# One more duo of F tiles in block products, and a new order of side work: a change to a two-layer convolution and pooling trunk

## The chip, the cores and the metric

The kernel runs on one core of one Trainium2 chip. The metric is device time of one execution in microseconds. The core has five engines that run their own instruction streams and wait for each other by semaphores: TensorE (PE: matmuls, and the weight loads PEld beside them), VectorE (DVE), ScalarE (ACT), GpSimd (POOL) and SyncE (SP). In this kernel SP issues most transfers; POOL's queue issues the rest, all those that add to what stands at their destination among them.

## The reference

Two residual layers over 1024 positions of 1024 channels, conditioned by a vector c. Each has a token mixer (layer 0: a causal convolution of width 31 with a gate and a layer norm; layer 1: pooled means) and a SwiGLU feed-forward part of width 2816.

```python
c_act = silu(c)
for i in range(2):
    sh_m, sc_m, g_m, sh_f, sc_f, g_f = split(c_act @ ada_w[i] + ada_b[i], 6)
    h = modulate(rms_norm(x, norm_mix_g[i]), sh_m, sc_m)
    y = conformer_conv(h, ...) if i == 0 else multiscale_pool(h, ...)
    x = x + (1 + g_m) * y
    h = modulate(rms_norm(x, norm_ffn_g[i]), sh_f, sc_f)
    x = x + (1 + g_f) * ((silu(h @ w_gate[i]) * (h @ w_up[i])) @ w_down[i])
return rms_norm(x, final_g)
```

All of it is float32. On the chip each operand of a large product is split in a high part (rounded to PE's fast float type) and a low part (the rest), and a product is three matmuls: high by high, high by low, low by high.

## The kernel before

**Tiling.** The sequence is cut in two chunks A and B of 512 positions; channels lie on the 128 partitions, so a tile is 128 x 512. F has 22 tiles, counted in 11 pairs `fp` (one gate and up product of 256 columns each) and 6 duos `q` (two pairs; the last has one). `products` (L506) issues the three matmuls of one product. `load_weight` (L489) loads a weight block, casts its high part on ACT and makes its low part on DVE or POOL or, with `summed`, as a negated copy on ACT to which a POOL transfer adds the block from memory.

**Block products.** The down product of the feed-forward part multiplies, for each duo, a 2 x 2 block matrix of weights (odd or even tiles, lower or upper half of the channels) with a 2 x 2 block matrix of activations (tiles by chunks). Instead of eight block products, seven are enough where sums and differences of blocks are formed first. Layer 1 does so for all duos. Layer 0 does it from pair `BEGINS[0]` on, which is 8: duos 4 and 5, F tiles 16 to 21. The tiles below are multiplied classically, the even tiles of chunk A already in the heads.

**Stages of layer 0.** (1) The first product of the convolution (`conv_in`), with the depthwise taps on DVE and POOL beside it (`Taps`, L800: POOL's share goes by a product on ACT and a sum on POOL). (2) The layer norm of chunk A (`layer_norm_silu`, L874), the second product `conv_out`, and the feed-forward norm of A (`norm`, L655; `modulated`, L645: a scaling on DVE, a high part on ACT, a low part on DVE, for each of eight channel tiles). Beside them `ada_columns` (L447) makes four of the modulation vectors of layer 0 by products of one column, a load of 512 KB for each of 32. (3) `heads` (L2024): two rounds of four pairs, each followed by a `down` (L1425) of A's even tiles, with the rest of B's taps and B's layer norm beside them. `gated` (L1061) applies the gate and splits the result. (4) `conv_out` of B and `all_joint` (L2042): for each pair the remaining head products, of which `joint` (L1212) ends each either by `gated`, which writes split tiles to memory, or by `paired` (L1268), which forms the operands of the block products and writes three blocks. (5) `first_down` (L1606): steps a and b (A's odd tiles, classical), p2, p1, p6, p7, p4, p5, p3 (block products), c to f (B, classical). Beside them run the pooling of layer 1 for A and the modulation of layer 1 (`ada_task`, L401).

**Side work of a block product step.** `weights` (L1639) forms and splits the weight block; `operand` (L1503) loads an activation block, casts the high part on ACT and subtracts it on DVE for the low part. `prepare` (L1679) loads operands four steps ahead and splits them two steps ahead; their parts stand in a ring of eight buffers (tag `h0`), two to a step.

**Order.** PE's order is the program's. For the other engines, work is emitted as tasks that `pace` (L234) steps while a model clock of DVE or POOL is less than 4 us ahead of PE's; `yield` names in `LOAD` and `DELAY` (L55, L71) say how long a task rests on that clock. A scheduler then orders each engine's instructions by priority and readiness, within the data's dependences and the added ones (`tc.add_manual_dep`), which here only fix an order on one engine.

## Time and profile before

| what | value |
|---|---|
| median of 3 runs | 1681.46 us (1680.39 to 1682.43) |
| the profiled execution | 1681.19 us, span 1679.4 us |
| PE busy | 1654.9 us, 99% of the span, 7550 matmuls |
| DVE busy | 1316.8 us, 78% |
| ACT busy | 805.0 us, 48% |
| POOL busy | 490.9 us, 29% |
| transfers | 378.60 MB, 225 GB/s |

Times inside the profile count from the start of the span. The chain of waits is followed back from the last instruction and gives each piece of the span to the engine that held it. In a timeline a row is a run of like instructions: start, length, engine, line, operation, output and inputs, count, and in brackets how long the engine stood before it and what ended that. Almost every instruction of DVE, ACT and POOL is issued by one helper and so has line L127, and every matmul L150; tiles tell them apart.

### The profile page before, as it was taken

Reading aid. Unit: us, or ns where it says so; the run is one execution under the profiler, and the core shown is the slowest. Engines: PE = TensorE matmul, PEld = TensorE weight load, DVE = VectorE, ACT = ScalarE, POOL = GpSimd, SP = SyncE. Lnnn points to the kernel's source line nnn. Section 1 sums busy time; section 2 is a strip of 40 time slices with the busy share of each in tenths; the row PEclk is TensorE's granted clock in tenths of the full one; section 3 lists DMA queues with packets and bytes.
Section 4 is the critical chain, followed back from the end, with each engine's and each line's share of the span. In section 5 each row is a group of like instructions: output and inputs, shape, how many; then the busy total and the mean of one; then the engine's idle time right before and its main releaser. Section 6 shows DMA issues by size and latency. Waiting matters only on the chain.

```text
span 1679.4 us, 21194 instructions
## 1 busy us (share of the span) xinstructions
PE 1654.9 (99%) x7550; PEld 1350.1 (80%) x7550; DVE 1316.8 (78%) x1866; ACT 805.0 (48%) x1091; POOL 490.9 (29%) x568
## 2 busy tenths in 40 slices
PE   7999999999999999999999999999999999999997
PEld 5777777778888888888888888888888888888887
DVE  8889899899758887888678957847877667658656
ACT  3669687867646332322224536637322222234354
POOL 3587767797001121211100502101111111000013
PEclk9999999999999999999999999999999999999999
DMA  8958997828677888887965959866777776686564
GB/s 302 287 181 223 225 240 205 226 76 239 203 232 182 269 267 299 259 272 219 389 236 159 288 168 269 244 215 202 197 222 223 213 233 185 202 276 210 184 169 126
DMA packets 117180, 378.60 MB, mean 225 GB/s; under 512 B 12369, under 2 KB 14545, under 8 KB 117074
## 3 DMA queue, kind: packets, MB, share of 16 engines
q1 hardware_dynamic: 79664, 245.63, 41.2%
q0 software_dynamic: 36832, 131.09, 32.3%
q8 instruction: 59, 0.97, 0.2%
q10 hardware_dynamic: 578, 0.53, 0.1%
q14 instruction: 47, 0.39, 0.1%
HBM read 310.61 MB, written 62.39 MB: 222 GB/s over the span
## 4 chain that ended last, share of the span: by engine, by line
PE 93%; DVE 3%; DMA 1%; POOL 1%; ACT 1%; issue 1%; SPq 0%; DVEq 0%; ACTq 0%; POOLq 0%
PE dn L150 25%; PE a L150 25%; PE e L150 14%; PE p L150 12%; PE y L150 6%; PE g L150 3%; PE first L150 3%; PE tap L150 2%; POOL pa L127 1%; PE ada L150 1%; DMA adaw<-in_adan_dram 1%; PE var L150 1%; DVE ca L127 0%; DVE u L127 0%; DVE v L127 0%
## 5 line engine op out<-in xcount | busy, mean ns | idle before, releaser
L127 ACT CAST w<-raw 128x1024 fp32r<-128x1024 f32 (+1 forms) x247 | 254.9, 1034 | 320.6 <-PE dn L150 61.5
L127 DVE TENSOR_TENSOR w<-raw,w 128x1024 fp32r<-128x1024 f32 (+1 forms) x173 | 210.0, 1218 | 58.9 <-ACT w L127 58.4
L150 PE MATMUL a<-n,w 128*128 128x512 f32 x1056 | 246.8, 389 | 0.2
L150 PE MATMUL p<-h,w 128*128 128x512 f32 x1056 | 244.2, 390 | 0.8 <-DVE h L127 0.6
L127 POOL TENSOR_TENSOR pa<-pa,pr 128x512 f32<-128x512 f32 x160 | 228.2, 1512 | 23.9 <-ACT pr L127 17.7
L150 PEld LDWEIGHTS p<-h,w 128*128 128x128 f32 x1056 | 197.3, 188 | 43.8 <-DVE h L127 1.5
L150 PEld LDWEIGHTS a<-n,w 128*128 128x128 f32 x1056 | 198.1, 188 | 42.1 <-DVE r L127 1.1
L150 PE MATMUL dn<-hi,w 128*128 128x512 f32 (+1 forms) x768 | 226.2, 377 | 0.5 <-DVE w L127 0.5
L150 PE MATMUL dn<-g,w 128*128 128x512 f32 x864 | 199.2, 390 | 1.4 <-DVE g L127 1.0
L150 PEld LDWEIGHTS dn<-g,w 128*128 128x128 f32 x864 | 161.8, 188 | 35.9 <-DVE g L127 1.3
L127 DVE SCALAR_TENSOR_TENSOR ca<-u,vecs,ca 128x512 f32<-128x512 f32 x245 | 169.7, 746 | 0.5
L150 PEld LDWEIGHTS dn<-hi,w 128*128 128x128 f32 x768 | 141.3, 188 | 26.9 <-DVE w L127 1.0
L150 PE MATMUL dn<-lo,w 128*128 128x512 f32 (+1 forms) x384 | 144.3, 376 | 0.0
L150 PE MATMUL a<-t,w 128*128 128x512 f32 x528 | 123.3, 389 | 0.0
L150 PE MATMUL e<-t,w 128*128 128x512 f32 x528 | 123.2, 389 | 0.0
L150 PE MATMUL e<-b,w 128*128 128x512 f32 x528 | 123.2, 389 | 0.0
L127 ACT ACTIVATE pr<-u,vecs 128x512 f32<-128x512 f32 x160 | 108.3, 717 | 25.3 <-POOL pa L127 17.5
L1144 POOL DMA_DIRECT2D raw<-in_wgu_dram x41 | 36.3, 885 | 278.7 <-DVE k L127 88.2
L150 PEld LDWEIGHTS a<-t,w 128*128 128x128 f32 x528 | 99.0, 188 | 20.7
L150 PEld LDWEIGHTS e<-t,w 128*128 128x128 f32 x528 | 99.1, 188 | 20.6
L150 PEld LDWEIGHTS e<-b,w 128*128 128x128 f32 x528 | 99.1, 188 | 20.6
L127 ACT CAST hi<-op 128x1024 fp32r<-128x1024 f32 (+1 forms) x52 | 48.5, 935 | 89.7 <-PE dn L150 80.9
(187 smaller groups left out, 2459.2 us busy)
## 6 DMA issues: line engine op xcount, KB each, us to landing
raw<-in_wgu_dram SPq DMA_DIRECT2D x132, 512.0 KB, 5.2
raw<-in_wds_dram SPq DMA_DIRECT2D x48, 512.0 KB, 5.7
adaw<-in_ada_dram POOLq DMA_DIRECT2D x48, 512.0 KB, 7.0
kinds<-k POOLq DMA_DIRECT2D x42, 512.0 KB, 7.9
raw<-in_wgu_dram POOLq DMA_DIRECT2D x41, 512.0 KB, 7.2
raw<-in_w_dram SPq DMA_DIRECT2D x36, 512.0 KB, 6.4
op<-kinds SPq DMA_DIRECT2D x36, 512.0 KB, 4.8
adaw<-in_adan_dram SPq DMA_DIRECT2D x32, 512.0 KB, 5.5
```

Source lines behind the costliest of these rows:

```text
L127: self.last = self.order(getattr(self.eng, name)(out, *args, **kw))
L150: last_mm[0] = nc.tensor.matmul(out, lhsT, rhs, start=start, stop=stop, skip_group_check=more).ins.name
L1144: d = order(nc.gpsimd.dma_start(w[i], wgu[l, fp, src], accum_op=ADD))
```

## The change

- `BEGINS[0]` is 6: pairs 6 and 7 (duo 3, F tiles 12 to 15) move to the block products. The heads' second round leaves out the upper half of their even tiles; the lower half stays there, so p2 is left out for this duo. `first_down` has three classical steps in a and b and twelve in c to f; its block weights come in other buffers, and block a22 is loaded when used, twice.
- In `operand`, with `added`, the low part is a negated copy on ACT, to which a POOL transfer adds the block from memory.
- `ada_columns` for vectors 4 and 5 does two columns at a time, every 9.5 us of the model clock instead of one every 4.0. `ada_task` goes by 2.0 instead of 6.0 from step b to step p4.
- Added orders: in the feed-forward norm of layer 0 scalings and low parts alternate; the convolution's gates, taps and some weight copies go behind the norm's parts, behind the layer norm's last parts, and behind the last head of the first round.
- The layer norm of B lets its root follow with shorter delays. `pool_end` of A follows step d instead of e.

```diff
-LOAD = {"load": 4.0, "slow": 6.0, "next": 4.0, "dots": 4.0}
+LOAD = {"load": 4.0, "brisk": 2.0, "both": 9.5, "slow": 6.0, "next": 4.0, "dots": 4.0}
...
-BEGINS = (8, 0)
+BEGINS = (6, 0)
...
@@ -67,6 +67,7 @@
 BESIDE = 12
 HOLD_TAPS = 4
 STRETCH = 1.2
+BEFORE_LOW = 8
 LATER = 300
 DELAY = {"stats": 2.75, "spread": 3.0, "soon": 0.5, "settled": 3.0, "later": 5.0, "root": 3.4}
 DELAY_BEHIND = {"stats": 8, "spread": 4, "soon": 0.5, "settled": 3.0, "later": 8}
...
@@ -450,16 +451,19 @@
         todo = [(j, k) for j in js for k in range(KT)]
         src = lambda j, k: adan[k, :, (j - 2) * D : (j - 1) * D]
         ws = [ada_load(src(*t)) for t in todo[:ADA_BUFS]]
-        for i, (j, k) in enumerate(todo):
-            yield "load"
-            if k == 0:
-                acc = bank("ada")
-            w = ws.pop(0)
-            for g in range(4):
-                matmul(acc[32 * g : 32 * g + 32, :Q], ccols[:, k, :], w[:, g * Q : g * Q + Q], start=k == 0, stop=k == KT - 1)
-            clock["PE"] -= 1.3
-            if i + ADA_BUFS < len(todo):
-                ws.append(ada_load(src(*todo[i + ADA_BUFS])))
+        n = 1 if js[0] == 2 else ADA_BUFS
+        for i in range(0, len(todo), n):
+            yield "both" if n > 1 else "load"
+            these = todo[i : i + n]
+            for j, k in these:
+                if k == 0:
+                    acc = bank("ada")
+                w = ws.pop(0)
+                for g in range(4):
+                    matmul(acc[32 * g : 32 * g + 32, :Q], ccols[:, k, :], w[:, g * Q : g * Q + Q], start=k == 0, stop=k == KT - 1)
+                clock["PE"] -= 1.3
+            for t in todo[i + ADA_BUFS : i + ADA_BUFS + n]:
+                ws.append(ada_load(src(*t)))
             if k == KT - 1 and (j != 3 or not held[0]):
                 yield from columns_done(j, acc)
             elif k == KT - 1:
...
@@ -492,8 +496,12 @@
         load(dst, src)
         wt = wts.tile([P, 2, D], F32R, tag="w", name=nm("w"))
         S_.copy(wt[:, 0, :n], raw)
+        copied = S_.last
         if summed:
             S_.activation(wt[:, 1, :n], raw, AF.Copy, scale=-1.0)
+            if "norm_a" in st and st.setdefault("first_summed", wt) is not wt:
+                tc.add_manual_dep(copied.ins, st["norm_a"][7][1].ins.name, edge, reason="behind the norm's high parts")
+                tc.add_manual_dep(S_.last.ins, st["norm_a"][7][1].ins.name, edge, reason="behind the norm's high parts")
             low = wt[:, 1, :n]
             order(nc.gpsimd.dma_start(low if len(src.shape) == 2 else low.rearrange("p (a b) -> p a b", a=src.shape[1]), src, accum_op=ADD))
             clock["G"] = max(clock["G"], clock["PE"]) + 1.0
...
@@ -501,6 +509,9 @@
         (V_ if st.get("own") or own else either(n)).tensor_tensor(wt[:, 1, :n], raw, wt[:, 0, :n].bitcast(F32), op=SUB)
         if st.get("own"):
             lows[id(wt)] = V_.last.ins, wt
+            if "kept_last" in st:
+                for ins, behind_it in zip((copied.ins, V_.last.ins), st.pop("kept_last")):
+                    tc.add_manual_dep(ins, behind_it, edge, reason="behind the last kept head")
         return wt
 
     def products(out, wt, k, act, first, last, o=0, n=None, more=False):
...
@@ -661,11 +675,18 @@
         else:
             rstd = yield from rms(ch, keep)
         quiet[0] = ffn and not l
+        made = []
         for k in range(KT):
             if k == HOLD_TAPS:
                 quiet[0] = False
-            modulated(ch, l, ffn, h, rstd, k)
+            made.append(modulated(ch, l, ffn, h, rstd, k))
+            if ffn and not l and k > 1:
+                tc.add_manual_dep(made[k][0].ins, made[k - 2][2].ins.name, edge, reason="two values behind")
+            if ffn and not l and k:
+                tc.add_manual_dep(made[k - 1][2].ins, made[k][0].ins.name, edge, reason="in turn")
             yield
+        if ffn and not l:
+            st["norm_a"], st["n_taps"] = made, 0
 
 
     units = []
...
@@ -720,6 +741,8 @@
         u = st["u", ch.i, p]
         sg = temp(ch.n, "acc", 2) if own else temp(ch.n)
         S_.activation(sg, bg, AF.Sigmoid, bias=V("conv_b1", KT + p))
+        if "v_high" in st:
+            tc.add_manual_dep(S_.last.ins, st.pop("v_high"), edge, reason="behind the layer norm's last high part")
         if ch.i == 0 and PE_TAPS.get(p) == CW:
 
             V_.scalar_tensor_tensor(ba, ba, V("conv_b1", p), sg, op0=ADD, op1=MUL)
@@ -732,6 +755,8 @@
             S_.copy(uhalo[:, p, :], ba[:, ch.n - HALO :])
             return
         V_.scalar_tensor_tensor(u[:, HALO:], ba, V("conv_b1", p), sg, op0=ADD, op1=MUL)
+        if "norm_a" in st:
+            tc.add_manual_dep(V_.last.ins, st["norm_a"][6][2].ins.name, edge, reason="behind the norm's first values")
         if ch.i == 0:
             V_.scalar_tensor_tensor(uhalo[:, p, :], ba[:, ch.n - HALO :], V("conv_b1", p), sg[:, ch.n - HALO :], op0=ADD, op1=MUL)
 
...
@@ -834,6 +859,13 @@
                         V_.tensor_scalar(self.acc, src, w(j), V("conv_bdw", p), op0=MUL, op1=ADD)
                     else:
                         V_.scalar_tensor_tensor(self.acc, src, w(j), self.acc, op0=MUL, op1=ADD)
+                    if "norm_a" in st and st["n_taps"] < BEFORE_LOW:
+                        st["n_taps"] += 1
+                        tc.add_manual_dep(V_.last.ins, st["norm_a"][6][2].ins.name, edge, reason="behind the norm's low parts")
+                    elif "v_low" in st:
+                        st["v_taps"] += 1
+                        if st["v_taps"] < BEFORE_LOW:
+                            tc.add_manual_dep(V_.last.ins, st["v_low"], edge, reason="behind the last low part")
                     twin = [t for t in tasks if isinstance(t, Taps)][:2]
                     if len(twin) == 2 and twin[0] is self:
                         i, k = (tasks.index(t) for t in twin)
...
@@ -907,7 +941,8 @@
                 tc.add_manual_dep(ins, V_.last.ins.name, edge, reason="behind the sums")
             recent.extend(beside[2:])
             beside.clear()
-        rstd = yield from mean_rsqrt(acc, n, when="settled" if ch.i else "stats", early=not ch.i)
+        fill = list(recent)
+        rstd = yield from mean_rsqrt(acc, n, when="soon" if ch.i else "stats", early=not ch.i, then="soon" if ch.i else None)
         S_.activation(tmp.tile([P, 16], F32, tag="col0", name=nm("col"), bufs=1)[:, 0:1], acc[:, 0:1], AF.Silu)
         hv = [pair(f"h{ch.i}", "v") for _ in range(KT)]
         sws = []
...
@@ -932,6 +969,10 @@
             yield
         if ch.i:
             low(KT - 1)
+        else:
+            st["v_low"], st["v_taps"] = V_.last.ins.name, 0
+            for ins in fill[BEFORE_LOW:]:
+                tc.add_manual_dep(ins, st["v_low"], edge, reason="behind the last low part")
         st["v", ch.i] = hv
 
     def conv_out(ch, squares, then=None):
...
@@ -1072,6 +1113,12 @@
                 return
         both = block("u0", "g")
         split(t, both, V_ if kept else None)
+        if kept and not l and f == 2 * ROUND - 2:
+            for ins in st["prs"]:
+                tc.add_manual_dep(ins, S_.last.ins.name, edge, reason="behind the last kept head")
+            for ins in beside[-3:]:
+                tc.add_manual_dep(ins, V_.last.ins.name, edge, reason="behind the last kept head")
+            st["kept_last"] = S_.last.ins.name, V_.last.ins.name
         if kept:
             st["g", i, f] = both[:, 0], both[:, 1]
         else:
...
@@ -1426,7 +1473,7 @@
 
         def half(d0, wd):
             def kept(take, give):
-                gs = [st["g", ch.i, f] for f in fs]
+                gs = [st["g", ch.i, f] for f in fs if not d0 or f // 2 < BEGINS[l]]
                 last = len(gs) - 1
                 todo = [range(4)] if not d0 else [range(2), range(2, 4)]
                 for ds in todo:
@@ -1438,7 +1485,7 @@
                             products(b, wd[i], d0 + d, g, i == 0, i == last)
                             if i == last:
                                 update(ch, d0 + d, b, gate_f, l)
-                        if ds is todo[-1] and d0:
+                        if ds is todo[-1] and (d0 or fs[i] // 2 >= BEGINS[l]):
                             give()
                         pace()
             return kept
...
-                sync.dma_start(raw[:, :w], kinds_d[l][q][b][:, :w, j])
+            sync.dma_start(raw[:, :w], source())
 
         def halves():
             raw = got["raw"]
             hi, lo = block("h0", "hi"), block("h0", "lo")
             S_.copy(hi[:, :w], raw[:, :w])
-            V_.tensor_tensor(lo[:, :w], raw[:, :w], hi[:, :w].bitcast(F32), op=SUB)
+            if added:
+                S_.activation(lo[:, :w], raw[:, :w], AF.Copy, scale=-1.0)
+                order(nc.gpsimd.dma_start(lo[:, :w], source(), accum_op=ADD))
+                clock["G"] = max(clock["G"], clock["PE"]) + 0.9
+            else:
+                V_.tensor_tensor(lo[:, :w], raw[:, :w], hi[:, :w].bitcast(F32), op=SUB)
             return [(hi[:, i], lo[:, i]) for i in range(w)]
 
         return load, halves
...
@@ -1618,35 +1673,27 @@
                 weight = wds[l, q, b] if ch.i and i % 2 == 0 else direct(wds[l, q, b])
                 steps.append((name, f"{name}{half}", i == 0, i == len(todo) - 1, [(ch, half)], weight, [(ch.i, f) for f in fs]))
 
-        def fetched_raw(name, b):
-            for q in (one, duo):
+        def wide(tag, name, q):
+            return block(tag, name, F32).rearrange("p a b -> p (a b)")[:, : duo_width(q) * 512]
+
+        def fetched_raw(name, b, tag):
+            for q in qs:
+                raw[q][name] = wide(tag, name, q)
                 d = nc.sync.dma_start(raw[q][name], wds[l, q, b][:, : duo_width(q) * 512])
                 tc.add_manual_dep(d.ins, last_mm[0], edge, reason="behind the products")
-
-        def first_blocks():
-            wide = [block("u0", "raw", F32).rearrange("p a b -> p (a b)") for _ in range(2)]
-            both = block("u0", "raw", F32)
-            raw[duo].update(a11=wide[0], a22=wide[1])
-            raw[one].update(a11=both[:, 0], a22=both[:, 1])
-            fetched_raw("a11", 0)
-            fetched_raw("a22", 3)
-
...
@@ -1659,11 +1706,12 @@
             return wt
 
         def seven(name, kind, of, key, fresh, ends):
-            for q in (one, duo):
-                steps.append((name, key, fresh and q == one, q == duo, ends, lambda q=q: weights(kind, q), operand(l, of, q)))
-
-        classical(A, range(duo), 0, ("odd",), "a")
-        classical(A, range(duo), 1, ("odd",), "b")
+            mine = [q for q in qs if kind != "a12" or q >= ROUNDS[l] * ROUND // 2]
+            for q in mine:
+                steps.append((name, key, fresh and q == mine[0], q == mine[-1], ends, lambda q=q: weights(kind, q), operand(l, of, q, True)))
+
+        classical(A, range(begins), 0, ("odd",), "a")
+        classical(A, range(begins), 1, ("odd",), "b")
         seven("p2", "a12", "b21", "y", True, [(A, 0)])
         seven("p1", "a11", "b11", "x", True, [(A, 0)])
         seven("p6", "s2", "t2", "x", False, [(B, 0)])
@@ -1671,9 +1719,9 @@
         seven("p4", "a22", "t4", "x", False, [(A, 1)])
         seven("p5", "s1", "t1", "y", True, [(B, 1)])
         seven("p3", "s4", "b22", "y", False, [(B, 0)])
-        for qs, names in ((range(duo // 2), "cd"), (range(duo // 2, duo), "ef")):
+        for some_qs, names in ((range(2), "cd"), (range(2, begins), "ef")):
             for half, name in enumerate(names):
-                classical(B, qs, half, ("even", "odd"), name)
+                classical(B, some_qs, half, ("even", "odd"), name)
         parts = [ops for *_, ops in steps if not isinstance(ops, list)]
 
         def prepare(upto):
...
@@ -2114,7 +2163,7 @@
         "b": lambda: unit(lambda take: lax.__setitem__(0, True)),
         "p1": lambda: pool_start(A),
         "p4": lambda: unit(lambda take: st.__setitem__("a_whole", True)),
-        "e": lambda: pool_end(A),
+        "d": lambda: pool_end(A),
     })
     need("norm_a")
     pool_start(B)
```

57 lines of the change are left out of this document (32 added, 25 removed).

## The prediction

> **What bounds the kernel now.** I read the page first, then the chain of waits, then windows by stage, then TensorE's (PE's) timeline round each place where it stands.
>
> ```profile
> span 1679.4 us, 21194 instructions
> PE 1654.9 (99%) x7550; PEld 1350.1 (80%) x7550; DVE 1316.8 (78%) x1866; ACT 805.0 (48%) x1091; POOL 490.9 (29%) x568
> PE 93%; DVE 3%; DMA 1%; POOL 1%; ACT 1%; issue 1%; SPq 0%; DVEq 0%; ACTq 0%; POOLq 0%
> ```
>
> The chain that ended last is 93% PE, so time comes off only where matmuls go away or where PE stands. What one matmul is worth is read in the chain where nothing disturbs it:
>
> ```profile
> 821.56 93.84 PE dn L150 x414
> ```
>
> 93.84 / 414 = 0.2267 us for a matmul of 512 columns, 24 of them 5.44 us. The windows say which other engine is close to full (columns: PE, weight loads, DVE, ACT, POOL, clock, DMA share, GB/s):
>
> ```profile
> 365.00:420.00 55.00, 55.00 (x245) 45.54 (x244) 53.82 (x68) 38.24 (x55) 44.14 (x33) 1.00 0.64 186
> 845.00:865.00 20.00, 20.00 (x90) 16.57 (x89) 9.49 (x14) 4.20 (x5) 0.53 (x1) 1.00 0.85 306
> 865.00:920.00 55.00, 55.00 (x249) 45.69 (x248) 48.22 (x71) 26.14 (x34) 2.75 (x11) 1.00 0.49 149
> 920.00:990.00 70.00, 70.00 (x312) 57.99 (x311) 53.43 (x79) 28.76 (x36) 23.04 (x37) 1.00 0.80 254
> ```
>
> PE is full in all four. DVE is at 98% in the head stage of the first layer, where the convolution's taps of the second half of the sequence run beside the heads, and at 88% in the block products (865 to 920).
>
> **The change part by part.**
>
> *Products.* With six pairs of F tiles done classically instead of eight, pairs 6 and 7 (duo 3) join the block products. In `first_down` steps a and b lose 24 matmuls each, c to f lose 96, and the duo brings 6 x 24 = 144 (its a12 product stays in the heads): 0 in sum. In the second round of heads the upper half of `down` loses two even tiles: 2 x 4 x 3 = 24 matmuls, 5.44 us. This is the sure term: -5.4.
>
> *Modulation in pairs.* The 16 column products of `ada_columns` (4, 5) are now issued two at a time. A single one costs this:
>
> ```profile
> 248.06 5.73 PE L150 MATMUL y<-v,w 128*128 128x512 f32 x24
> 253.72 0.64 PE L150 MATMUL ada<-adaw,ccols 128*32 128x256 f32 x8
> 254.29 16.62 PE L150 MATMUL y<-v,w 128*128 128x512 f32 x72
> ```
>
> From 248.06 to 253.72 are 5.66 us for 24 matmuls worth 5.44, so going into and out of a group costs 0.22 us beside the group's own 0.57. Eight pairs instead of sixteen singles save 8 x 0.22 = 1.8 us; nothing if PE then waits for the second load of a pair. That load has two units of about 5.7 us, as before, so I take 1.8.
>
> *Stalls that the orders aim at.* PE's timeline at the layer norm of the first half, the FFN norm, and the first round of heads:
>
> ```profile
> 244.82 1.52 PE L150 MATMUL y<-v,w 128*128 128x512 f32 x6
> 246.83 0.50 PE L150 MATMUL y<-v,w 128*128 128x512 f32 x1 [0.48 <-DVE v L127]
> 304.24 3.13 PE L150 MATMUL p<-h,w 128*128 128x512 f32 x13
> 307.70 1.66 PE L150 MATMUL p<-h,w 128*128 128x512 f32 x6 [0.33 <-DVE h L127]
> 309.68 0.73 PE L150 MATMUL p<-h,w 128*128 128x512 f32 x2 [0.32 <-DVE h L127]
> 357.68 2.65 PE L150 MATMUL dn<-g,w 128*128 128x512 f32 x11
> 360.79 0.50 PE L150 MATMUL dn<-g,w 128*128 128x512 f32 x1 [0.45 <-ACT g L127]
> 362.26 2.11 PE L150 MATMUL dn<-g,w 128*128 128x512 f32 x8 [0.97 <-DVE g L127]
> ```
>
> From start to start, less 0.2267 a matmul: 244.82 to 246.83 loses 0.65; 304.24 to 307.70 and on to 309.68 lose 0.51 and 0.62; 357.68 to 360.79 and on to 362.26 lose 0.62 and 1.24. Each last stall of a place is followed by a restart that costs 0.11 more, the half of the 0.22 above. So 0.8 + 1.2 + 2.0 = 4.0 us. At the FFN norm DVE's order shows the cause:
>
> ```profile
> 300.98 1.41 DVE L127 SCALAR_TENSOR_TENSOR t<-x,gains,rstd 128x512 f32<-128x512 f32 x2 [2.51 <-PE rstd L150]
> ...
> 304.93 2.05 DVE L127 SCALAR_TENSOR_TENSOR t<-x,gains,rstd 128x512 f32<-128x512 f32 x3
> 306.90 0.74 DVE L127 SCALAR_TENSOR_TENSOR h<-t,mod,h 128x512 fp32r<-128x512 f32 x1
> 307.57 0.74 DVE L127 SCALAR_TENSOR_TENSOR u<-a,vecs,acc 128x512 f32<-128x512 f32 x1
> ```
>
> Three scalings run ahead of the third low part, and a convolution gate (u) ahead of the fourth. In turn, and with the gate behind, the third low part ends 2 x 0.66 us sooner and PE's wait of 0.5 goes. The price is the gate: put behind eight scalings and seven low parts of some 0.66 from 301.0 on, it ends at about 311.6 instead of 308.3, and the PSUM banks that it reads come free later. If the second head's banks are among these, PE, which comes to that head at about 310, waits up to 2 us; the trace doesn't say which bank is whose. Bounds 0 to 2; I take 0, since two banks of the norm's root are also returned there. In the heads, taps step behind the casts and splits; their work is only moved, and what is late next is the taps, which feed the sums below.
>
> *What is late next: the layer norm of the second half.* PE reaches its mean sooner by 1.8 + 4.0 = 5.8 us.
>
> ```profile
> 416.31 0.68 DVE L127 TENSOR_TENSOR acc<-acc,u 128x512 f32<-128x512 f32 x1
> 422.02 1.02 PE L150 MATMUL mean<-acc,ones 128*128 128x512 f32 x2
> 434.69 0.69 DVE L127 SCALAR_TENSOR_TENSOR acc<-t,acc 128x512 f32<-128x512 f32 x1
> 436.50 0.95 PE L150 MATMUL var<-ones,acc 128*128 128x1 f32 x8
> 441.48 1.05 PE L150 MATMUL rstd<-ident,col 128*128 128x128 f32 x8
> 449.81 2.49 DVE L127 TENSOR_TENSOR v<-t,v 128x512 fp32r<-128x512 f32 x4
> 455.13 43.68 PE L150 MATMUL y<-v,w 128*128 128x512 f32 x192
> ```
>
> The sum is done at 417.0 and DVE is full ahead of it, so it does not come sooner by itself: of 5.8 us only 5.0 are there, and 0.8 comes back as a wait for the mean (between 0, if DVE's idle slots close with PE, and 5, if the moved taps make the sum as late as PE gains). From mean to the first y are 33.1 us, with 24 matmuls fewer 27.7. The first low part of v is ready at 450.4, 28.4 behind the mean: 0.7 too late. But the change lets the root's two products go 1.1 us (436.50 against 435.4) and about 2.2 us sooner, by delays "soon" instead of "settled" and "root". That leaves 2.6 us of slack; a product placed before its sum costs at most the 1.1 again. I take 0.
>
> *Side work of the block products.* Twenty operand steps instead of fourteen. On each the DVE's low part goes, and ACT makes a negated copy, and a POOL DMA adds the operand from memory:
>
> ```profile
> L127 DVE TENSOR_TENSOR lo<-op,hi 128x512 fp32r<-128x512 f32 (+1 forms) x12 | 11.4, 953 | 1.3 <-ACT hi L127 1.2
> L127 ACT ACTIVATE w<-raw 128x1024 fp32r<-128x1024 f32 x9 | 9.5, 1052 | 0.0
> L498 POOL DMA_DIRECT2D w<-in_wds_dram x8 | 7.2, 901 | 105.0 <-ACT w L127 98.0 <-PE var L150 6.6 <-issue 0.4
> w<-in_wds_dram POOLq DMA_DIRECT2D x8, 512.0 KB, 7.2
> w<-in_wdg_dram POOLq DMA_DIRECT2D x6, 512.0 KB, 9.2
> POOL adaw L175 <- DVE adaw L127: 48.5, 11, 15.5
> ```
>
> DVE loses some 14 x 0.95 = 13 us; ACT gains 20 of up to 1.05 = 21 us over 90, and was half idle. The question is latency. The operand ring holds four steps, so step n+2 can be split when n-2 ends, three steps (12 + 24 + 24 matmuls, 13.6 us) ahead of its use. The way is high copy 1.05, negated copy 1.05, issue 0.9, landing 7.2: 10.2 us, or 12.2 with the slowest landing (9.2). Both fit, so nothing; I take 1 us for one step at the seam at about 854, where the products now begin 10.9 us sooner (48 matmuls less ahead of them) while the DMA share is 0.85. Bounds 0 and 13 (below). The extra loads (six operands, a22 twice) go into a stretch with a share of 0.49.
>
> The Trainium skill speaks against this edit: "SBUF — State Buffer", section "SBUF: two separate sides", says that a POOL-issued transfer cannot write its descriptors while DVE holds the port pair the two share, about 620 ns becoming about 3100. By that ratio the issue of 0.9 would be an estimated 4.5 us, the way 13.8, and 0.2 us a wide step, some 3 us, would be lost. The 901 ns above are a mean beside a DVE that is 76% busy (920 to 990), so this trace does not show it.
>
> *Pooling behind.* The first half is whole after p4, now 48 matmuls later:
>
> ```profile
> 969.51 0.69 DVE L127 TENSOR_TENSOR mx<-win,mx 128x512 fp32r<-128x512 f32 x1
> 988.68 3.56 PE L150 MATMUL y<-mx,w 128*128 128x512 f32 x15
> ```
>
> Its slack of 18.5 us shrinks by 10.9 to 7.6: nothing. Modulation dots that ran there are brought forward by "brisk", which lightens it. The joint units of pairs 6 and 7 write block operands instead of split ones, which pairs 8 to 10 already do with PE full: nothing.
>
> *Sum.* -5.4 - 1.8 - 4.0 + 0.8 + 1.0 = -9.4. The profiled execution took 1681.2 us (span 1679.4 and 1.8 round it; the median of the runs is 1681.5, the same within 0.02%). Forecast: 1681.2 - 9.4 = 1671.8.
>
> **The rivals.**
>
> *DVE bounds the head stage.* The reorders only move DVE's work, the sum of the second half stays the last thing, and the 4.0 + 1.8 in front of it are lost at the mean. For it: 53.82 of 55 us. Against: 5.0 us between sum and mean now. Only the 24 matmuls are left: 1681.2 - 5.4 = 1675.8.
>
> *The additive transfers come too late* (slower). POOL's queue is in order, and the modulation's loads stand in it until DVE has done a dot: 48.5 us in 11 waits, 4.4 each, in the last row of that fence. A transfer queued behind one has a way of 10.2 + 4.4 = 14.6 us against 13.6, and "brisk" calls for dots in just this stage. It decides from 3.4 us of lateness on. If it hits all 13 wide steps at 1.0 us: +13, 1684.8; with the landing of 9.2 as well 3.0 x 13 = 39, 1711. Against it: the scheduler places a dot when its data should be there, and the DMA share is low in this stage.
>
> *The same, milder.* Each issue has to wait out what DVE is doing:
>
> ```profile
> L127 DVE TENSOR_TENSOR w<-raw,w 128x1024 fp32r<-128x1024 f32 (+1 forms) x173 | 210.0, 1218 | 58.9 <-ACT w L127 58.4
> ```
>
> Three such splits in a row, 3.7 us, would be 0.3 over the limit: 13 x 0.3 = 4, 1675.8. Against it stands the issue's mean of 901 ns beside a busy DVE. It is the page's rule as this kernel would meet it.
>
> *It does not pay.* The matmuls go, but the gate's banks (2.0), the mean (5) and the seam (several us) take it back: 1681.2 - 11.2 + 10 = 1680. For it: all three lie at places where PE has no slack now. Against: they would have to come together.
>
> **How the numbers follow.** Chances: forecast 0.58 (1669 to 1675), DVE-bound 0.16, late transfers 0.11 and their milder form 0.04, no pay 0.11. From no change a measurement of this kernel tells about 0.2%, 3.4 us, so faster means under 1678.1 and slower over 1684.8. Faster: 0.58 + 0.16 + 0.04 less 0.02 for their tails, 0.76; same: 0.13, the case without pay and those tails; slower: 0.11. The lower end is all gains with no return, 1681.2 - 11.2 = 1670.0, less 2.0, the spread of the three runs shown (1680.4 to 1682.4), and 1.0, one more stall of the size of those above: 1667. The upper end takes in the DVE-bound case, the milder one and the case without pay: 1681.
>
> **What would show it.** Right: 24 fewer `dn` matmuls before the last heads; the ada groups of 16 matmuls, eight of them; no wait of `p` on DVE h, of `y` on DVE v, of `dn` on g; `mean` starting at about 417. Wrong: PE waiting in `dn` for the operand's low part or for DMA between 850 and 945; `mean` waiting for acc by more than 3 us; `p` waiting for u at 310; y of the pooled part waiting for mx. Most would be lost if POOL's rows show additive issues idle behind DVE adaw.

## The result, and the profile after

The changed kernel takes **1706.2 us** (median of 4 runs, 1705.7 to 1708.6) against 1681.9 for the kernel before beside it: ratio 1.0145, 95% interval 1.0133 to 1.0157. It is 24 us slower, where 9.4 us faster was forecast. From the page of the profiled execution, the span and the chain that ended last:

```profile
span 1704.7 us, 21178 instructions
...
PE 82%; issue 5%; DMA 4%; DVE 4%; POOL 4%; ACT 2%; SPq 0%; DVEq 0%; POOLq 0%; ACTq 0%
```

PE carried 93% of that chain before and 82% now: other engines and transfers hold it up. PE's timeline first shows the places where nothing went wrong (line numbers are one higher in this kernel: L151 for matmuls, L128 for the helper of the other engines):

```profile
300.67 4.92 PE L151 MATMUL p<-h,w 128*128 128x512 f32 x21
305.52 1.07 PE L151 MATMUL ada<-adaw,ccols 128*32 128x256 f32 x16
306.52 4.64 PE L151 MATMUL p<-h,w 128*128 128x512 f32 x19
...
354.66 9.79 PE L151 MATMUL dn<-g,w 128*128 128x512 f32 x42
...
434.80 1.05 PE L151 MATMUL var<-ones,acc 128*128 128x1 f32 x8 [0.58 <-DVE acc L128]
...
446.29 3.96 PE L151 MATMUL y<-v,w 128*128 128x512 f32 x16 [1.00 <-DVE v L128]
...
812.54 2.65 PE L151 MATMUL dn<-g,w 128*128 128x512 f32 x11
```

The stalls at 307 to 309 and at 360 are gone, the modulation comes 16 matmuls at a time, and the first `dn` of `first_down` starts at 812.54; in the trace of before it starts at 821.40. So far 8.9 us are gained. The windows of the stages behind it (columns as in the prediction) show where they are lost:

```profile
813.00:845.20 32.20, 32.20 (x144) 26.66 (x143) 19.52 (x28) 8.62 (x10) 5.24 (x10) 1.00 1.04 382
845.20:969.00 123.80, 104.46 (x409) 82.69 (x408) 76.03 (x109) 58.53 (x74) 32.73 (x55) 0.90 0.91 246
969.00:1013.70 44.70, 43.85 (x194) 35.99 (x193) 29.96 (x43) 14.37 (x17) 11.05 (x13) 1.00 0.68 186
```

The middle row is the block products: 396 matmuls of 512 columns, worth 396 x 0.2267 = 89.8 us, take 123.9 (845.18 to 969.07 in the trace; the count of 409 in the row holds a few short products too). All 34 us are there. The DMA share is the mean busy share of the 16 DMA engines; 0.51 in the block products before, it is 0.91 here. The granted clock is 0.90. What PE waits for in them (us, times, longest):

```profile
PE dn L151 <- DMA lo<-kinds: 11.3, 4, 3.6
PE var L151 <- DVE acc L128: 4.0, 1, 4.0
PE dn L151 <- DVE x L128: 3.7, 4, 1.6
PE dn L151 <- ACT w L128: 1.2, 1, 1.2
```

That is 20 us of idle time; the largest part are waits for additive transfers to land (`lo<-kinds`, the operands' low parts). The rest is lost behind the waits:

```profile
861.27 0.61 PE L151 MATMUL dn<-hi,w 128*128 128x512 f32 x2
864.48 0.79 PE L151 MATMUL dn<-lo,w 128*128 128x512 f32 x1 [2.60 <-DMA lo<-kinds]
865.07 1.05 PE L151 MATMUL dn<-hi,w 128*128 128x512 f32 x2
865.93 0.63 PE L151 MATMUL dn<-lo,w 128*128 128x512 f32 x1
866.35 1.05 PE L151 MATMUL dn<-hi,w 128*128 128x512 f32 x2
867.21 0.63 PE L151 MATMUL dn<-lo,w 128*128 128x512 f32 x1
867.63 0.67 PE L151 MATMUL dn<-hi,w 128*128 128x512 f32 x2
868.15 0.40 PE L151 MATMUL dn<-lo,w 128*128 128x512 f32 x1
```

From 865.07 to 867.63 six matmuls take 2.56 us, 0.427 each, and then 0.23 again: half clock after the stall. Counted from start to start over the stage, 45 matmuls go at half clock and lose 9.0 us, the four landings 11.9, the `var` product 4.2, and the updates, restarts and short products the remaining 9.0 of 34.1.

### The profile page after: what moved, and what is told of

Same layout as the page of the kernel before. It is cut to its first block, busy times and chain, and to the rows that moved or that the text cites. A ratio compares the mean times of both kernels' runs of the same rounds, so it can differ in the third digit from the quotient of the medians.

```text
span 1704.7 us, 21178 instructions
## 1 busy us (share of the span) xinstructions
PE 1661.0 (97%) x7526; PEld 1354.2 (79%) x7526; DVE 1309.0 (77%) x1861; ACT 820.0 (48%) x1108; POOL 504.5 (30%) x587
## 4 chain that ended last, share of the span: by engine, by line
PE 82%; issue 5%; DMA 4%; DVE 4%; POOL 4%; ACT 2%; SPq 0%; DVEq 0%; POOLq 0%; ACTq 0%
PE a L151 24%; PE dn L151 19%; PE e L151 14%; PE p L151 10%; PE y L151 6%; POOL pa L128 3%; PE first L151 3%; PE g L151 2%; PE tap L151 2%; DMA adaw<-in_ada_dram 1%; DMA lo<-kinds 1%; DVE u L128 1%; DMA adaw<-in_adan_dram 1%; PE ada L151 1%; DVE acc L128 1%
## 5 line engine op out<-in xcount | busy, mean ns | idle before, releaser
L128 ACT CAST w<-raw 128x1024 fp32r<-128x1024 f32 (+1 forms) x239 | 246.8, 1035 | 254.1 <-DMA raw<-in_wgu_dram 58.4
L151 PE MATMUL dn<-hi,w 128*128 128x512 f32 (+1 forms) x864 | 264.3, 388 | 4.5 <-DVE x L128 2.8
L151 PE MATMUL a<-n,w 128*128 128x512 f32 x1056 | 246.8, 389 | 0.2
L151 PE MATMUL p<-h,w 128*128 128x512 f32 x1056 | 244.4, 391 | 0.0
L128 DVE TENSOR_TENSOR w<-raw,w 128x1024 fp32r<-128x1024 f32 (+1 forms) x167 | 203.4, 1222 | 44.4 <-ACT w L128 44.3
L128 POOL TENSOR_TENSOR pa<-pa,pr 128x512 f32<-128x512 f32 x159 | 226.9, 1512 | 28.4 <-ACT pr L128 23.1
L151 PEld LDWEIGHTS a<-n,w 128*128 128x128 f32 x1056 | 198.0, 188 | 42.2 <-DVE r L128 1.1
L151 PEld LDWEIGHTS p<-h,w 128*128 128x128 f32 x1056 | 197.2, 188 | 42.6 <-DMA w<-in_wgu_dram 0.9
L151 PEld LDWEIGHTS dn<-hi,w 128*128 128x128 f32 x864 | 164.3, 194 | 38.5 <-DVE x L128 4.1
L151 PE MATMUL dn<-lo,w 128*128 128x512 f32 (+1 forms) x432 | 167.9, 389 | 11.3 <-DMA lo<-kinds 11.3
L128 DVE SCALAR_TENSOR_TENSOR ca<-u,vecs,ca 128x512 f32<-128x512 f32 x246 | 170.6, 746 | 0.5
L151 PE MATMUL dn<-g,w 128*128 128x512 f32 x696 | 160.7, 390 | 1.1 <-DVE x L128 1.1
L151 PEld LDWEIGHTS dn<-g,w 128*128 128x128 f32 x696 | 130.3, 188 | 29.4 <-DVE x L128 1.9
L151 PE MATMUL a<-t,w 128*128 128x512 f32 x528 | 123.3, 389 | 0.0
L151 PE MATMUL e<-b,w 128*128 128x512 f32 x528 | 123.2, 389 | 0.0
L151 PE MATMUL e<-t,w 128*128 128x512 f32 x528 | 123.2, 389 | 0.0
L128 ACT ACTIVATE pr<-u,vecs 128x512 f32<-128x512 f32 x159 | 108.3, 717 | 24.9 <-POOL pa L128 19.9
L151 PEld LDWEIGHTS a<-t,w 128*128 128x128 f32 x528 | 99.1, 188 | 20.7
L151 PEld LDWEIGHTS e<-b,w 128*128 128x128 f32 x528 | 99.1, 188 | 20.6
L151 PEld LDWEIGHTS e<-t,w 128*128 128x128 f32 x528 | 99.1, 188 | 20.6
L128 ACT CAST hi<-op 128x1024 fp32r<-128x1024 f32 (+1 forms) x58 | 54.9, 947 | 115.8 <-PE dn L151 107.4
```

The source lines that it names most:

```text
L128: self.last = self.order(getattr(self.eng, name)(out, *args, **kw))
L151: last_mm[0] = nc.tensor.matmul(out, lhsT, rhs, start=start, stop=stop, skip_group_check=more).ins.name
```

## The experiments

Four theories go by letters in the expectations. **A** or **L**: the additive way (two copies, POOL's queue, landing) is too long for the ring of four steps. **Q**: POOL's queue stands behind modulation loads that wait for dots. **D**: the third duo, or DVE's work and its waits, overfills the stage. **T**, formed after the first four runs: the DMA engines are full. Diffs are against the changed kernel unless another is named; `...` marks what is left out. The times of the block products are read in each trace, from their first matmul to the next classical `dn`.

### The low parts by DVE again, and the dots' pause

```diff
-... operand(l, of, q, True)))
+... operand(l, of, q)))
```

> The changed kernel with one part undone: the block products' operand low parts are again made by DVE (low = operand minus its high part) and not by a negated copy and an additive transfer; all else as changed. The changed kernel loses 34 us in its block products (396 matmuls worth 89.8 us take 123.9). Theory A, the additive way is too long (copies, POOL's queue, a landing of 9 to 12 us instead of 7.2, against the 13.6 us that the ring of four steps allows): the loss goes, 1706 - 34 + 1 to 4 for DVE's twenty lows of 0.95 us, so 1671 to 1677. Theory D, the third duo of pairs with the brisk modulation dots is what overfills the stage, whatever makes the low part: DVE gets 19 us more and it stays at 1695 or more. Theory Q, POOL's queue blocked behind modulation loads: as theory A here, because nothing of the operand stands on POOL any more.

Measured: 1682.2 us, ratio 1.0001 (0.9991 to 1.0010); block products 97.7 us. So the additive transfers cost 24 us. The block products still take 8 us more than 89.8, which is why A's forecast (1671 to 1677) is missed.

```diff
-LOAD = {... "brisk": 2.0, ...}
+LOAD = {... "brisk": 6.0, ...}
```

> The changed kernel with the pause between modulation dots in the block products back at 6.0 from 2.0 (fewer modulation loads of 512 KB on POOL's queue in this stage), the additive transfers kept. Theory Q, the additive issues stand behind modulation loads that wait for DVE's dots: most of the 34 us goes, 1675 to 1685. Theory A, the way is too long by itself: the DMA share falls a little, landings shorten by 1 to 2 us, and a third of the loss at most goes, 1693 to 1706; dots left over then stand in the pooled part and may take 2 to 5 us there.

Measured: 1704.8 us, 1.0130 (1.0105 to 1.0154), block products 124.9. The pause is not it. But nine modulation loads are issued in the stage in both runs, so theory Q is not settled by this one.

With both edits:

> Both undone: low parts by DVE, and the pause of the dots back at 6.0. If A or Q holds, the block products are as free as in the run with DVE's lows alone, so within 2 us of that run in this stage; against it the last modulation dots come later and the pooling, which has some 8 us of slack by the forecast, may lose up to 5 us: 1671 to 1681. If D holds through the dots, it is faster than the run with DVE's lows alone by 10 us or more.

Measured: 1683.9 us, 1.0012 (1.0001 to 1.0022), block products 97.2: as with DVE's lows alone in this stage, with six modulation loads instead of nine. D through the dots would have made it 10 us faster.

The kernel before, with the additive way for its fourteen operands:

```diff
...
-            V_.tensor_tensor(lo[:, :w], raw[:, :w], hi[:, :w].bitcast(F32), op=SUB)
...
+            S_.activation(lo[:, :w], raw[:, :w], AF.Copy, scale=-1.0)
+            order(nc.gpsimd.dma_start(lo[:, :w], source(), accum_op=ADD))
...
```

> The kernel before, with the additive way alone: its fourteen operand low parts by a negated copy and a POOL transfer that adds, nothing else of the change. Theory A: each of the wide steps loses 1 to 3 us and more with the half clock behind the long stalls, some 10 to 25 us, 1692 to 1706. Theory Q: the pause of the dots is 6.0 here, so few loads stand ahead of the additive issues and it loses 0 to 5 us, 1681 to 1687. Theory D: no loss, or a gain of up to 1 us from DVE's lighter load, 1680 to 1682.

Measured: 1689.7 us, 1.0041 (1.0026 to 1.0056): +7.5, under A's band and over Q's. The additive way loses with two duos as well, though less: its block products take 64.6 us instead of 58.5, and PE waits for a low part only once, for 0.7 us.

### Way or throughput

```diff
+            if not l and st["ring"] % 5 == 4:
...
+                hi, lo = st["fifth"]
+            else:
                 hi, lo = block("h0", "hi"), block("h0", "lo")
...
-            while counts[1] < min(upto + SPLIT, len(parts)):
+            while counts[1] < min(upto + SPLIT + 1, len(parts)):
```

> The changed kernel with a ring of five operand steps instead of four (a fifth pair of buffers from free blocks, the split one step earlier), the additive transfers kept: the way may take 4 steps, some 19 us, instead of 13.6. Theory L, the way is only too long (its landings of 9 to 12 us): the waits for low parts (11.9 us and the half clock behind them) go, 1706 - 16 or more, at most 1690. Theory T, the DMA engines are what is full: in the block products of the changed kernel they were busy 0.91 of 123.8 us, 112.7 us, for work in which the matmuls take 89.8; a longer ring moves nothing of that, the stage stays at 110 us or more, the landings get longer by what the ring gained, and the time stays at 1693 or more.

Measured: 1704.9 us, 1.0135 (1.0115 to 1.0155), block products 123.6. A third more time for the way brings 1 us. That does not make the way short. The traces give it for each of the 18 operands in and just ahead of this stage, from the start of the high copy to the landing. In the changed kernel it is 15.4 us in the mean, over 13.6 for 12 of the 18, and 16.6, 18.9, 23.8 and 22.3 us for the four that PE waits for. What is longest in it is a wait that no expectation names:

```profile
858.76 1.05 ACT L128 ACTIVATE lo<-op 128x1024 fp32r<-128x1024 f32 x1
864.54 1.05 ACT L128 ACTIVATE lo<-op 128x1024 fp32r<-128x1024 f32 x1
...
867.39 1.12 POOL L1571 DMA_DIRECT2D lo<-kinds  x1 [2.09 <-issue]
...
877.04 9.85 DMA lo<-kinds
...
896.64 9.38 DMA lo<-kinds
```

The first two rows are the negated copies of two operands; they end at 859.81 and 865.59. Their transfers are issued at 867.39 and 877.04 (the last two rows are pieces of the chain of waits, from an issue to its landing). So they stand in POOL's queue for 7.6 and 11.4 us. The second is issued 0.32 us after the first has landed, at 876.72. It is so throughout: of twelve wide transfers (512 KB) of operands, ten are issued 0.31 to 0.34 us after the landing of an earlier transfer of POOL's queue, mostly the wide one before. In none of the eight traces with additive transfers of operands are two wide ones of them under way together. The standing is 4.5 us in the mean of the 18, up to 12.4. With five steps in the ring it is 8.2 in the mean, up to 17.2: the time that the ring gives is spent in the queue. The measured time is as T forecast it (1693 or more), the landings are not: T had them longer, and the wide ones take 7.7 us in the median instead of 8.6.

This gives an estimate of its own. Two wide operands and a narrow one go with 60 matmuls, 13.6 us. Two wide transfers one behind the other take 13.6 us at a landing of 6.5, as at 914 and 930 in this trace, and 19.4 at 9.4, the median of the five issued between 854 and 897. In the kernel before, with the additive way, there is one wide transfer for 36 matmuls, 8.2 us, and its landing takes 8.1: it about fits, and the issues stand 0.6 us in the mean.

```diff
-                order(nc.gpsimd.dma_start(lo[:, :w], source(), accum_op=ADD))
+                order(nc.gpsimd.dma_start(lo[:, :w].bitcast(F32), source()))
```

> The changed kernel with the additive transfers made plain: the same POOL queue, the same bytes, the same copies ahead of them, but the operand overwrites the negated copy instead of being added to it, so the low part is the whole operand and the block products are not those of the reference. By the two traces at hand a MB on POOL's queue takes 5.6 us of all sixteen DMA engines when it is added and 3.3 when it is plain, so 8.2 MB would free 19 of 112.7 us. Theory T (DMA engines full, adding costs double): share down to about 0.85, landings 2 us shorter, waits for low parts under half of 11.9, 1683 to 1697. Theory L (copies, queue and any landing on POOL's queue): waits as before, 1700 or more.

Measured: 1684.7 us, 1.0017 (1.0006 to 1.0027), block products 101.6: 21.5 of the 24 us go when the same bytes on the same queue are not added. That adding is the cause is shown by this. Two things go away with it. The first is the standing: every issue follows its copy by 0.4 to 0.7 us, up to four transfers of POOL's queue are under way, two wide ones among them, and the way is 9.0 us in the mean and 12.5 at most. The second is work of the DMA engines. Their queues in the block products, with DVE's lows, changed, and with plain transfers (packets, MB, share of 16 engines; q0 is POOL's; in the rows of transfers: count, KB each, median us to landing):

```profile
q1 hardware_dynamic: 5842, 15.59, 46.8%
q0 software_dynamic: 1505, 5.51, 18.6%
...
raw<-in_wds_dram SPq DMA_DIRECT2D x10, 512.0 KB, 5.3
```

```profile
q0 software_dynamic: 5735, 13.67, 51.5%
q1 hardware_dynamic: 6313, 16.72, 39.6%
...
lo<-kinds POOLq DMA_DIRECT2D x12, 512.0 KB, 8.6
raw<-in_wds_dram SPq DMA_DIRECT2D x10, 512.0 KB, 7.6
...
lo<-kinds POOLq DMA_DIRECT2D x5, 256.0 KB, 10.5
```

```profile
q1 hardware_dynamic: 6313, 16.73, 45.2%
q0 software_dynamic: 3848, 13.80, 39.5%
...
lo<-kinds POOLq DMA_DIRECT2D x12, 512.0 KB, 6.8
raw<-in_wds_dram SPq DMA_DIRECT2D x11, 512.0 KB, 7.0
...
lo<-kinds POOLq DMA_DIRECT2D x6, 256.0 KB, 5.5
```

The shares are of windows of 97.7, 123.8 and 104.8 us. POOL's queue keeps the sixteen engines busy 18.2 us without the operands, 63.8 with added ones and 41.4 with plain ones. By the differences, 8.2 MB cost 45.6 us added, **5.6 us a MB**, and 8.3 MB 23.2 us plain, 2.8 us a MB: adding doubles the price. The weights' loads on SP's queue land in 7.6 us beside added transfers, 7.0 beside plain ones and 5.3 with neither, so most of their delay comes with the bytes and not with the adding.

The Trainium skill ("DMA: Bandwidth & Descriptors", section "Anatomy of one DMA — SWDGE (gpsimd) path") gives 2.0 us and the bytes at 436 GB/s for one transfer on this path, an estimated 3.2 us for 0.52 MB; measured in this stage are 6.8 plain and 8.6 added, so that figure is no guide where the share is 0.85 to 0.91.

### Loads or dots

```diff
+                if "brisk" in st:
+                    V_.tensor_copy(mod[:, b : b + 1], w[:, 0:1])
+                else:
                     ada_dot(w, l, j, k)
```

> The changed kernel, additive transfers and all, with the same dots left out and their loads kept. Rival D, DVE stands head-of-line behind late modulation loads and its updates come late by that: most of its part of the loss goes, 1706 - 10 or more, 1696 or less. Theory T (the DMA engines' time): the transfers stay as many, the waits for low parts stay, 1699 or more.

Measured: 1708.7 us, 1.0162 (1.0142 to 1.0183), block products 126.3. Then the loads out as well:

```diff
+                if w is None:
+                    V_.tensor_copy(mod[:, b : b + 1], cact[:, 0:1])
...
-                    ws.append(ada_load(ada[(l * 6 + j2) * KT + k2], soft))
+                    ws.append(None if "brisk" in st else ada_load(ada[(l * 6 + j2) * KT + k2], soft))
```

> As the run before it, with the loads of these dots left out too: 12 transfers of 0.52 MB at 3.3 us a MB, some 20 of the 112.7 us of the DMA engines. Theory T: the waits for low parts shrink with it, 12 to 22 us faster than the run with the loads kept, 1680 to 1690. Rival D and theory L: within 5 us of that run.

Measured: 1693.6 us, 1.0073 (1.0050 to 1.0096), block products 109.3. Without the dots nothing is gained; without their loads 15 us are, within the 12 to 22 that theory T gave as the difference (the time itself is 4 over its band) and three times what D and L allowed. These loads are more than bytes, though. They also stand in POOL's queue, and DVE stands for them: 17.8 us in the changed kernel, and 9.7 even without the dots, because the copy in a dot's place waits for the same load. Without the loads all three are gone together; the issues of the additive transfers stand 3.5 us in the mean instead of 5.5. Q in its own form falls: they stand as long without dots, and most of them behind landings. The windows of the two:

```profile
845.20:969.00 123.80, 101.02 (x399) 79.06 (x399) 70.19 (x106) 59.61 (x75) 36.22 (x57) 0.92 0.92 251
```

```profile
845.20:955.00 109.80, 98.90 (x412) 79.09 (x411) 71.31 (x107) 59.56 (x76) 32.85 (x48) 0.95 0.92 232
```

The share is 0.92 in both: the stage shrinks with its transfers.

| kernel | block products, us | DMA engines busy, share x window, us |
|---|---|---|
| changed | 123.9 | 112.7 |
| ring of five | 123.6 | 110.2 |
| additive, no dots | 126.3 | 113.9 |
| additive, no dots, no loads | 109.3 | 101.0 |
| additive, dots earlier (below) | 118.5 | 99.6 |
| plain transfers | 101.6 | 89.1 |
| DVE's lows | 97.7 | 64.5 |

In the first five the transfers need more than the 89.8 us of the matmuls, as T has it. But their sum is only a floor: the stage is 8 to 19 us longer than it, and the fourth and fifth rows differ by 9 us with about the same sum. With plain transfers (in a window 3 us longer than the stage) the transfers need just as much as the matmuls, and with DVE's lows less; there 8 to 12 us are lost to something else.

How full engines and the queue share the 24 us is **not shown**: no run takes away one and leaves the other. The traces fit both together. Where PE waits for low parts in the changed kernel, 861 to 906 us, the share is 0.97 and most wide landings take 9 to 10 us, and the queue adds these landings up. From 906 to 929 the share is 0.81 and wide landings take 6.6 to 8.2 us; two of the three wide transfers there still stand, for 7 and 10 us, but PE waits for no low part.

### What is left without the additive transfers

```diff
-... operand(l, of, q, True)))
+... operand(l, of, q, q == begins)))
```

> The changed kernel with the additive transfer for the third duo's operands alone (six steps of 512 KB) and DVE's low parts for the other two: DMA engines 64.5 + 6 x 2.9 = 82 us of some 95, DVE 6 us lighter than with its lows alone. Theory T: both fit, the block products lose 2 to 7 us, 1675 to 1682. Theory L: each of the six is late by 2 to 3 us and half of them meet the half clock, 12 to 20 us beside DVE's 7: 1690 or more.

Measured: 1683.5 us, 1.0006 (0.9997 to 1.0016), block products 97.9; PE does not wait for a low part there, and the issues stand 1.0 us in the mean. Six additive transfers fit, as T has it and as the queue has it (one wide one for 60 matmuls), and bring nothing either: a little over T's band.

```diff
+                if "brisk" in st:
+                    V_.tensor_copy(mod[:, b : b + 1], w[:, 0:1])
+                else:
                     ada_dot(w, l, j, k)
...
-... operand(l, of, q, True)))
+... operand(l, of, q)))
```

> DVE's low parts, and the modulation dots that fall into the block products are left out (their loads still run; a column copied from the load stands in for each sum, so the second layer's modulation is not the reference's). DVE loses ten or more dots of 1.22 us, 12 us or more of 85. If DVE's fullness makes the 7 us lost there: 2 us at most stay, 1675 to 1678. If late operands do: 1680 to 1683.

Measured: 1688.4 us (three runs, 1682.6 to 1689.3), 1.0032 (1.0012 to 1.0052), block products 106.9, and DVE busy 76.4 us of a window of 99.5. With a lighter DVE the stage is no shorter: DVE's fullness alone does not make these 8 us. With DVE's lows again, the next run has two edits, in the block products and in the layer norm of the second half:

```diff
-    V_.tensor_tensor(mine["s4"], mine["s4"], mine["s2"], op=ADD)
+    G_.tensor_tensor(mine["s4"], mine["s4"], mine["s2"], op=ADD)
...
-        rstd = yield from mean_rsqrt(acc, n, when="soon" if ch.i else "stats", early=not ch.i, then="soon" if ch.i else None)
+        rstd = yield from mean_rsqrt(acc, n, when="settled" if ch.i else "stats", early=not ch.i)
```

> DVE's low parts, the old delays of the root in the second half's layer norm, and the three s4 additions on POOL, with the pauses of the changed kernel. From 1682: the additions take 3 us and up to 3.6 us of head-of-line waiting off DVE in the block products, the delays 1 us of stalls at the layer norm. If DVE's fullness makes the 7 us: 1676 to 1679, and the third duo pays a little. If single late operands make it, or POOL's additions (some 3 us each) are late for p3: 1680 to 1684.

Measured: 1691.8 us, 1.0068 (1.0051 to 1.0085). Its block products take 97.2 us, as before the edit. Of the 10 us, 8.5 are lost ahead of `first_down`, to the delays (next section). What PE waits for in the block products of all runs with DVE's lows are updates of `x` in DVE's queue, 3.3 to 4.6 us in each (in three of them 3.5 us for a sum of squares besides). One from the run with DVE's lows alone:

```profile
868.79 0.47 PE L151 MATMUL dn<-hi,w 128*128 128x512 f32 x1 [1.07 <-DVE x L128]
```

The next product goes on in the same four banks of PE's output, so it waits until DVE has read them, and something stands ahead of the update in DVE's order. What it is differs from run to run (a weight's load, a copy that waits for the ring), for every edit gives the planner another order. Which late operand makes the 8 us **stays open**.

```diff
-LOAD = {... "slow": 6.0, ...}
+LOAD = {... "slow": 5.0, ...}
```

> DVE's low parts as in the run with these alone, and the pause between modulation dots outside the block products 5.0 instead of 6.0, so that some six more of the 47 dots are done in the joint stage ahead, where DVE is 80 to 85% busy under a full PE. In the block products DVE (85 of 98 us) gets 7 us lighter and 3 MB less come over POOL's queue. If DVE's fullness and its head-of-line waits make the 7 us that are lost there: 1682 - 4 to 6, 1676 to 1678. If the waits are for single late operands whatever DVE has to do: 1680 to 1683. If the joint stage is too full for more dots, slower than 1683.

Measured (with DVE's lows): 1704.7 us, 1.0143 (1.0128 to 1.0158). It missed what it aimed at: PE waits 11.4 us in the joint stage for DVE's `r`, five times, and `first_down` starts at 830.1 instead of 812.8. DVE is no busier there than in the run with DVE's lows alone (144.4 against 146.4 of 180 us). But it stands 17.9 us for modulation loads that have not landed, eight times, and in that run not at all. So late data differs between the two, and not DVE's work. The same with the s4 additions on POOL:

> As the run before it, and the three additions that make the weights s4 go to POOL (the elementwise engine, not its DMA queue) instead of DVE: DVE loses 3 us of work and its waits for the late load of a12 (3.6 us in the run with DVE's lows alone, 5.8 with additive transfers for the third duo). 1 to 3 us faster than that run, 1674 to 1677, if those waits are what delays the updates; the same if POOL's additions of some 3 us each are late for p3; slower by 2 or more if POOL and DVE hinder each other at what they share.

Measured: 1701.5 us, 1.0127 (1.0110 to 1.0144). And with the additive transfers:

> The changed kernel, additive transfers and all, with the pause of 5.0 outside the block products: some six modulation loads fewer there, 3 MB at 3.3 us a MB of the DMA engines, 10 of 112.7 us, and 7 us of DVE. Theory T (DMA engines full): what is lost falls by about what they are relieved of, 1706 - 8 to 14, 1692 to 1698. Theory L (the way is too long in itself): 1702 or more.

Measured: 1718.3 us, 1.0224 (1.0209 to 1.0239). The joint stage loses 14 and 19 us in these two, so neither decides what it was made for; the last one's block products do fall, from 123.9 to 118.5.

### The orders without the duo

```diff
-BEGINS = (6, 0)
+BEGINS = (8, 0)
...
-... operand(l, of, q, True)))
+... operand(l, of, q)))
```

> The changed kernel without the third duo (the classical products begin at eight pairs again, as before) and with DVE's low parts: what stays of the change are the modulation in pairs, the side orders and the brisk dots. The forecast's terms for these: -1.8 - 4.0 + 0.8, so 1681.7 - 5.0 = 1677; the 24 matmuls (-5.4) are not in it. If the block products with two duos run without loss, as before, this gives 1676 to 1679; if the run with DVE's lows alone (1682) lost its 7 us to the brisk dots or to the second load of a22 and not to the third duo, this loses as much and ends at 1682 to 1685.

Measured: 1684.9 us, 1.0020 (1.0011 to 1.0030), though its block products take 59.6 us, 1.1 more than before. The loss is at the second half's layer norm:

```profile
431.80 1.86 PE L151 MATMUL var<-ones,acc 128*128 128x1 f32 x8 [2.37 <-DVE acc L128]
433.52 3.76 PE L151 MATMUL dn<-g,w 128*128 128x512 f32 x8
```

With 24 matmuls more behind the mean than in the changed kernel, the delays "soon" put the product 2.4 us ahead of its sum, and eight matmuls behind it take 3.76 us: half clock. With the old delays (the edit of `mean_rsqrt` above):

> The run with the orders alone, with one of these orders undone: the two products of the root in the second half's layer norm go behind the old delays again. In the run with the orders alone PE stood 2.4 us there for the sum of squares, ran eleven matmuls at half clock behind it (2.2 us) and waited 1.6 us more for the root's copy. If that placement is what cost the orders their gain, this gives back 4 to 6 us of 1684.9: 1679 to 1681, and 1677 if all the forecast's terms hold. If the sum of squares is late whatever the placement (DVE full), it stays at 1683 or more.

Measured: **1678.4 us, 0.9989 (0.9980 to 0.9999)**, the one version that comes out ahead of both kernels: 1.8 us ahead of the kernel before by the ratio, 2.9 by the medians, and its interval only just leaves out no change. The stall is gone:

```profile
418.46 14.21 PE L151 MATMUL dn<-g,w 128*128 128x512 f32 x60
432.51 0.95 PE L151 MATMUL var<-ones,acc 128*128 128x1 f32 x8
433.32 0.96 PE L151 MATMUL dn<-g,w 128*128 128x512 f32 x3
```

And the old delays with 24 matmuls fewer, in the run with s4 on POOL, come too late for the `y` behind them:

```profile
447.13 0.50 PE L151 MATMUL y<-v,w 128*128 128x512 f32 x1 [2.84 <-ACT v L128]
451.00 11.27 PE L151 MATMUL y<-v,w 128*128 128x512 f32 x38 [3.36 <-DVE v L128]
```

So the delay and the count of matmuls belong together. The first pair of runs differs by 6.6 us at the start of `first_down` (824.0 against 817.5), the second, with DVE's lows, by 8.5 (821.3 against 812.8 with "soon"): that is what each mismatch costs.

## Why the prediction was wrong

- **Products, modulation in pairs, stalls (-5.4, -1.8, -4.0): right.** At the second round of heads (`p`, 375.77 before, 369.56 after) 6.2 us are gained, 5.8 were forecast for pairs and stalls; the 24 matmuls are gone too, so this part of the forecast held by its mechanism.
- **The mean of the second half (+0.8), the layer norm behind it (0): low by 1.5.** `mean` does not wait, but `var` by 0.58 and `y` by 1.00 us. At `first_down` 8.9 us were gained, 10.4 forecast.
- **Side work of the block products (+1.0): this step failed; the stage lost 34.** It asked a right question, whether the way of 10.2 us fits in 13.6, and had the way wrong. It added up two copies, the issue and one landing, and put the standing in POOL's queue behind transfers of the same kind at nothing. Measured are a standing of 4.5 us in the mean and up to 12.4, a landing of 8.6 instead of 7.2 (10.5 for the narrow ones), and a way of 15.4 in the mean, 16.6 to 23.8 where PE waits. Plain transfers, which do not stand, have a way of 9.0. The step also asked for one transfer and not for the rate of twenty. It put only "six operands, a22 twice" into the stretch with a share of 0.49, and left the additive transfers themselves out of that account: 8.2 MB at 5.6 us a MB, 45.6 us of the engines' time beside the 64.5 of the run with DVE's lows, 110 in a stage of 89.8. Undoing the transfers brings 24 us, and the third duo without them keeps 8 (below). That adding is dear stood in the queues of the whole trace before only as a hint: POOL's queue took 23.0% of the engines for 10.49 MB between 822 and 990 us, SP's 49.7% for 30.28 MB, 3.7 against 2.8 us a MB.

```profile
q1 hardware_dynamic: 9954, 30.28, 49.7%
q0 software_dynamic: 2880, 10.49, 23.0%
```

- **The price of a stall.** The forecast counted a stall at its length and a restart of 0.11 us. In the changed kernel 9.0 of 34 us are matmuls at half clock behind stalls.
- **The third duo without additive transfers** loses 8 us in the block products, where the seam's 1 us was taken. Its 24 matmuls (5.4) do not pay for that: DVE's lows give 1682.2, no gain. Which late operand it is, stays open.
- **The rival "additive transfers come too late"** (0.11, 1684.8 to 1711) named the place, POOL's queue, and held the time. Its mechanism was half right: the transfers do stand in that queue until the way is over 13.6 us, but behind landings of earlier transfers and not behind dots. Without the dots the time stays (1708.7) and so does the standing (5.5 us); without their loads, 3.5 us of standing remain. Its milder form, an issue that takes longer beside DVE, is not borne out: 17 issues took 1.1 us in the median, 1.3 at most. **"Brisk"**, taken as a relief, cost nothing: 1704.8 without it.
- **Pooling behind, the slack of 7.6:** it was not seen as a bound; in the third window above PE stands 0.85 us.

## What to carry to other kernels

Before moving work from an engine to DMA, ask for the rate and not only for the latency of one transfer. Sum up the DMA engines' time of the stage (share x length, and each transfer by its us a MB) against its matmul time, with an accumulating transfer at twice a plain one, as measured here. Then sum up the landings of the large accumulating transfers one behind the other against the same time. In the trace, compare when a transfer's data is ready with when it is issued: a wait there is no engine's busy time. When matmuls are taken from between two dependent products, their planned delays have to move with them.

## What the hardware showed that was not expected

**Adding in a DMA** took 5.6 us of sixteen engines a MB, plain 2.8.

**Large additive transfers of one queue went one at a time.** No two wide ones of operands were under way together in eight traces, and 10 of 12 in the changed kernel were issued 0.31 to 0.34 us after an earlier landing; the same transfers without the addition were issued 0.4 to 0.7 us after their copies and overlapped. What holds the issue is not shown: the profile names no wait for it, or an instruction that was done long before.

**Half clock behind short stalls.** In the eighteen traces, behind 300 us, 41 of 43 stalls of PE of 2.2 us and more are followed within 45 matmuls by 5 to 16 starts 0.40 to 0.46 us apart instead of 0.2267 (by 7 to 12 in 33 of them); of 83 stalls of 0.7 to 1.8 us, 14 are. At 0.2 us for each such start, a stall costs 1 to 3 us more than its length. The Trainium skill ("TensorE: Matmul & The Clock Gate", section "Part 1: The HAM clock gate (the "warmup" mystery)") puts the half clock behind an idle window of about 3.4 us and lets some 3.4 us of work bring the full clock back. The way back agrees in size, 7 to 12 matmuls at 0.427 are 3.0 to 5.1 us; the way in does not, since stalls of 2.3 to 2.8 us were enough here.
